# Query projections in the keys' form with evacuation by heads, and a reordered second row of the values, in a two-layer decoder trunk

## The chip, the cores and the metric

The kernel runs on one core of a Trainium2 chip. The metric is the device time of one execution in microseconds (us). Five engines work side by side, each through its own instructions in order: TensorE (PE, with its weight loads listed apart as PEld) for matrix products, ScalarE (ACT), VectorE (DVE), GpSimd (POOL) and SyncE (SP), which issues the loads. The trace gives the granted clock of TensorE as 0.998 of its full 2.4 GHz over the whole span.

## The reference, cut to what matters

Two pre-norm residual layers over 256 positions of width 1024: the first mixes tokens by attention with 8 heads of 128, the second by a causal pooling; each is followed by an MLP. With 256 positions there is one key block, so the attention is plain causal attention:

```
xn  = rms_norm(x, norm_mix[0])
q, k, v = split(xn @ w_qkv)          # 8 heads of 128 each
q, k = rotate the first 32 channels of each head by position (k likewise)
p   = softmax(mask(q @ k.T / sqrt(128)))
x   = x + (p @ v) @ w_o
x   = x + relu(rms_norm(x) @ w_up)**2 @ w_down
```

All inputs and outputs are float32.

## The kernel before

**Products in parts.** Each float32 matrix operand is split into a high part, rounded to the type that TensorE multiplies at full rate, and a low part, the rest. A product is three products: high by high, high by low, low by high. Weights come in slabs of 128x2048 (1 MB), each loaded by SyncE into one of three buffers `raw_*`, then split in pieces: ScalarE copies a piece (`wh_*`, line 177), VectorE subtracts (`wl_*`, line 181). `pump(n)` issues n such pieces, first the copy, then the subtraction; `pump_h` and `pump_l` issue the copies or the subtractions alone; `use(kind, j)` makes sure that a slab's pieces have been issued. After the last subtraction of a slab, the load of the slab three later is issued into the buffer that has come free. The slabs in order: four of the values, then for each of four pairs of heads keys and queries, then four of the output projection, then the MLP's.

**The order.** The order on each engine is written out by hand. What the program names first on an engine runs first there; between engines only data and buffers hold an instruction back.

**Values (lines 506 to 560).** Row k of eight: the tokens' channels k are transposed by TensorE (`transposes`), scaled into a high part by ScalarE and a low part by VectorE (lines 328, 333), and multiplied with row k of the value weights into four banks `dv`, 12 products of 512 columns. Within a row the steps run over (n, h): n is the kind of the three products, h the half of 512 columns. The dictionary `ahead` says at which row the transposes for later rows are issued.

**Attention (lines 588 to 756).** For each pair of heads j: the keys' products, their evacuation with the rotation, the scores of pair j - 1 (from the second pair on), then the queries' products, their evacuation, and the transposes of the probabilities of pair j - 1. The keys of pairs 1 to 3 are made by `wide_lo` and `wide_hi`: one head has a bank of its own, whose columns 0 to 255 take the products with the tokens' high part and 256 to 511 those with their low part, so that one product of 512 columns serves both; `key_evac` adds the halves. The queries, and the keys of pair 0, are made by `chan_block`: 24 products of 256 columns for each head, both heads in one bank; `qk_evac` shuffles the rotating channels into `sw` (line 598), multiplies the bank by the cosine table (599), `sw` by the sine table (601) and adds the two (602). Lines 601 and 602 run on VectorE for pair 0 and the queries of pair 1, on GpSimd otherwise.

**Scores and after.** `scores` (line 629) makes two score banks, adds the mask on VectorE (640), takes the exponentials on ScalarE (648), and scales the rows by the reciprocal sums: head 0 on ScalarE (656), head 1 on VectorE (659). `prob_t` transposes the probabilities on TensorE, `attend` multiplies them with the values; its result is split into `ah` (ScalarE, 709) and `al` (VectorE, 710). The score banks, the transposed probabilities and the results of `attend` take turns in two PSUM banks of tag "t": a bank is written again when its last reader is done. The queries' banks have the tag "u", also two.

Of the kernel before, what the change touches and what calls it, by code (L numbers as in the profile page):

```python
# [84 lines left out]
def tile_trunk(ctx: ExitStack, tc: tile.TileContext, x_in, positions, norm_mix, norm_mlp,  # L85
# [132 lines left out]
    def pump(n):  # L218
        for _ in range(n):
            hi_step()  # L220
            while lows:
                lo_step()
# [132 lines left out]
    def both(pair):  # L355
        pair[0]()
        pair[1]()
# [145 lines left out]
    nc.vector.tensor_scalar(xs[:, 0, 0:SEQ], t0[:, 0:SEQ], gcol[:, 0:1], None, op0=ALU.mult)  # L503
    lo()
    pump_h(1)
    ahead = {0: (1, 1), 1: (2, 2), 3: (4, 2)}
    for k in range(KT):
        wh, wl = use("v", k // 2, 99 if k % 2 else (2 if k < 4 else 1))
        ev = transposes(ahead[k][0], 0, "a", n=ahead[k][1]) if 0 < k and k in ahead else None
        steps = [(n, h) for n in range(3) for h in range(2)]  # L510
        if k == 0:
            steps.sort(key=lambda nh: nh[1])
        for n, h in steps:
            if k == 0 and (n, h) == (0, 1):
                both(transposes(1, 0, "a", n=1))
            hs = slice(h * HALF, (h + 1) * HALF)
            for s in range(NS):
                x0 = (SEQ if n == 1 else 0) + s * P
                w = wl if n == 2 else wh
                nc.tensor.matmul(dv[s, h], xs[:, k, x0:x0 + P], w[:, k % 2, hs],  # L520
                                 start=k == 0 and n == 0, stop=k == KT - 1 and n == 2)
# [1 line left out]
            block_split(6)  # L523
            block_split(7)
        if k < 7:
            pump(2 if k < 3 else 1)
        if k == 4:
            block_turn(6)
            block_turn(7)
# [63 lines left out]
    def qk_evac(nm, j, u):  # L593
        ct, st = tab[nm]
        t = work.tile([P, 2, SEQ], F32, tag="X", name="t_%s_%d" % (nm, j), bufs=4)
        sw = work.tile([ROT, 2, SEQ], F32, tag="sw", name="sw_%s_%d" % (nm, j), bufs=2)
        uv = u.rearrange("p (f t) -> p f t", f=2)
        nc.vector.stream_shuffle(sw.rearrange("p f t -> p (f t)"), u[0:ROT, :], swap)
        nc.vector.tensor_tensor(t, uv, ct.broadcast_to([P, 2, SEQ]), op=ALU.mult)
        e = nc.vector if j == 0 or (nm, j) == ("q", 1) else nc.gpsimd  # L600
        e.tensor_tensor(sw, sw, st.broadcast_to([ROT, 2, SEQ]), op=ALU.mult)
        e.tensor_tensor(t[0:ROT], t[0:ROT], sw, op=ALU.add)
        return t
# [5 lines left out]
    def key_evac(j, us):  # L609
# [10 lines left out]
        e.tensor_tensor(t, t, ct.broadcast_to([P, 2, SEQ]), op=ALU.mult)  # L620
        e.tensor_tensor(sw, sw, st.broadcast_to([ROT, 2, SEQ]), op=ALU.mult)
        e.tensor_tensor(t[0:ROT], t[0:ROT], sw, op=ALU.add)
        return t

    qk = {}
# [3 lines left out]
    def scores(j):  # L629
# [22 lines left out]
        for a in range(2):  # L652
            for b, (c0, c1) in enumerate(((0, P), (P, 3 * P))):
                i = 2 * a + b
                if a == 0:
                    nc.scalar.activation(pr[a][:, c0:c1], pr[a][:, c0:c1], AF.Copy,
                                         scale=sums[:, i:i + 1])
                else:
                    nc.vector.tensor_scalar(pr[a][:, c0:c1], pr[a][:, c0:c1],
                                            sums[:, i:i + 1], None, op0=ALU.mult)  # L660
        prob[j] = pr

    pts = {}
# [52 lines left out]
    for j in range(4):  # L716
# [24 lines left out]
            qk["k", j] = key_evac(j, us)  # L741
            scores(j - 1)
        w = use("q", j)
        u = qk_bank("q", j)
        chan_block(u, w, 0)
        pump(1 if j else 2)
        chan_block(u, w, 1)
        qk["q", j] = qk_evac("q", j, u)
        if j == 0:
            pump(1)  # L750
        if j == 3:
            nc.scalar.activation(vh, vsb[:, 0, HALF:D], AF.Copy)
            nc.vector.tensor_tensor(vl, vsb[:, 0, HALF:D], vh.bitcast(F32), op=ALU.subtract)
# [440 lines left out]
```

## Time and profile before

| | us |
|---|---|
| median of 3 runs | 484.26 |
| lowest, highest | 484.18, 484.8 |
| profiled execution | 484.62 |
| its span, first to last instruction | 482.5 |

The span is that of one execution in the hardware profiler. A page of the profile gives busy times of the engines, the span in slices, the chain of work that ended last, followed back from the last instruction, and groups of instructions by line. Beside the page the trace answers questions: timelines of an engine, tables of busy time by stretch, the chain in order of time, and waits. Matrix products are pipelined, and their ends are modelled: where products follow each other, the distance from start to start is what one costs. A name in a row is that of the program without its number, so `wl_k` stands for the keys' slabs of all pairs.

### The profile page before, as it was taken

How to read it: one execution, taken by the hardware profiler on the slowest of the kernel's cores; microseconds unless marked ns; L12 is line 12 of the kernel's file. 1: busy time of each engine (PE TensorE's matmuls, PEld its weight loads, DVE VectorE, ACT ScalarE, POOL GpSimd, SP SyncE). 2: the span in 40 equal slices, each digit the busy share in tenths (PEclk: the TensorE clock that was granted, in tenths of full speed). 3: DMA queues.
4: the chain of work that ended last, by engine and by line, in shares of the span. 5: the costliest groups of instructions: out<-in, count | busy, mean ns of one | idle time of the engine just before them, and what ended most of it. 6: DMA issues, size and time to landing. Idle time of an engine off the chain costs nothing.

```text
span 482.5 us, 6552 instructions
## 1 busy us (share of the span) xinstructions
PE 474.7 (98%) x2570; PEld 412.1 (85%) x2570; DVE 338.8 (70%) x498; ACT 255.1 (53%) x418; POOL 43.1 (9%) x41
## 2 busy tenths in 40 slices
PE   8999999999999999999999999999999999999994
PEld 7789999888888888888888889888888888888884
DVE  4789998955877484848566687778756557484745
ACT  4696665653686272635355554476535446272523
POOL 6910456300000000000000000000000000000000
PEclk9999999999999999999999999999999999999999
DMA  7986643480477758556573570078747472736202
GB/s 266 349 280 223 196 174 123 143 259 1 124 251 236 263 196 282 186 163 219 170 249 147 175 261 2 18 248 297 239 135 277 139 252 97 262 120 230 88 1 87
DMA packets 57342, 89.58 MB, mean 186 GB/s; under 512 B 2944, under 2 KB 46048, under 8 KB 57312
## 3 DMA queue, kind: packets, MB, share of 16 engines
q1 hardware_dynamic: 56896, 88.72, 55.1%
q8 instruction: 20, 0.33, 0.3%
q10 hardware_dynamic: 416, 0.45, 0.3%
q14 instruction: 10, 0.08, 0.0%
HBM read 88.11 MB, written 1.05 MB: 185 GB/s over the span
## 4 chain that ended last, share of the span: by engine, by line
PE 97%; DMA 1%; SPq 0%; ACT 0%; DVE 0%; issue 0%; ACTq 0%
PE u_m L432 24%; PE u_m L425 13%; PE d_m L401 12%; PE d_m L402 12%; PE d_m L403 12%; PE d_v L520 4%; PE k L432 2%; PE u_q L411 2%; PE u_q L410 2%; PE u_q L415 2%; PE d_o L401 2%; PE d_o L403 2%; PE d_o L402 2%; DMA xt<-in_x_dram 1%; PE k L425 1%; PE d_p L1066 1%
## 5 line engine op out<-in xcount | busy, mean ns | idle before, releaser
L432 PE MATMUL u_m<-xs,wh_u 128*128 128x512 f32 x512 | 122.1, 390 | 0.0
L432 PEld LDWEIGHTS u_m<-xs,wh_u 128*128 128x128 f32 x512 | 94.7, 188 | 18.8
L401 PE MATMUL d_m<-wh_d,hh 128*128 128x512 f32 x252 | 98.1, 389 | 0.0
L402 PE MATMUL d_m<-wl_d,hh 128*128 128x512 f32 x252 | 98.0, 389 | 0.0
L403 PE MATMUL d_m<-wh_d,hl 128*128 128x512 f32 x252 | 98.0, 389 | 0.0
L181 DVE TENSOR_TENSOR wl_d<-raw_d,wh_d 128x1024 fp32r<-128x1024 f32 x64 | 76.2, 1221 | 17.0 <-ACT wh_d L177 17.0
L181 DVE TENSOR_TENSOR wl_u<-raw_u,wh_u 128x1024 fp32r<-128x1024 f32 x64 | 75.8, 1222 | 12.2 <-ACT wh_u L177 12.2
L177 ACT ACTIVATE wh_d<-raw_d 128x1024 fp32r<-128x1024 f32 x64 | 64.7, 1046 | 21.7 <-DMA raw_d<-in_mlp_w_down_dram 21.7
L799 ACT ACTIVATE t<-u_m 128x256 f32<-128x256 f32 x64 | 24.0, 378 | 83.8 <-PE u_m L425 54.6
L177 ACT ACTIVATE wh_u<-raw_u 128x1024 fp32r<-128x1024 f32 x64 | 63.9, 1046 | 7.1 <-DMA raw_u<-in_mlp_w_up_dram 7.1
L425 PEld LDWEIGHTS u_m<-xs,wl_u 128*128 128x128 f32 x512 | 64.0, 191 | 1.4
L425 PE MATMUL u_m<-xs,wl_u 128*128 128x256 f32 x512 | 64.9, 283 | 0.0
L800 DVE TENSOR_TENSOR t<-u_m,t 128x256 f32<-128x256 f32 x64 | 26.5, 422 | 53.9 <-ACT t L799 53.2
L403 PEld LDWEIGHTS d_m<-wh_d,hl 128*128 128x128 f32 x252 | 47.3, 188 | 9.8
L401 PEld LDWEIGHTS d_m<-wh_d,hh 128*128 128x128 f32 x252 | 47.3, 188 | 9.8
L402 PEld LDWEIGHTS d_m<-wl_d,hh 128*128 128x128 f32 x252 | 47.3, 188 | 9.8
L810 ACT ACTIVATE hh<-hf 128x512 fp32r<-128x512 f32 x32 | 20.2, 633 | 45.0 <-DVE hf L809 45.0
L811 DVE TENSOR_TENSOR hl<-hf,hh 128x512 fp32r<-128x512 f32 x32 | 22.2, 692 | 22.5 <-ACT hh L810 22.5
L809 DVE SCALAR_TENSOR_TENSOR hf<-t 128x512 f32<-128x512 f32 x32 | 22.1, 692 | 1.1
L410 PE MATMUL u_q<-xs,wh_q 128*128 128x256 f32 x64 | 18.6, 291 | 0.0
L411 PE MATMUL u_q<-xs,wl_q 128*128 128x256 f32 x64 | 18.1, 283 | 0.0
L415 PE MATMUL u_q<-xs,wh_q 128*128 128x256 f32 x64 | 18.1, 283 | 0.0
(218 smaller groups left out, 554.8 us busy)
## 6 DMA issues: line engine op xcount, KB each, us to landing
raw_u<-in_mlp_w_up_dram SPq DMA_DIRECT2D x32, 1024.0 KB, 6.3
raw_d<-in_mlp_w_down_dram SPq DMA_DIRECT2D x32, 1024.0 KB, 4.8
raw_o<-in_attn_w_o_dram SPq DMA_DIRECT2D x4, 1024.0 KB, 4.8
raw_k<-in_attn_w_qkv_dram SPq DMA_DIRECT2D x4, 768.0 KB, 5.2
raw_q<-in_attn_w_qkv_dram SPq DMA_DIRECT2D x4, 768.0 KB, 4.8
raw_v<-in_attn_w_qkv_dram SPq DMA_DIRECT2D x2, 1024.0 KB, 9.0
raw_v<-in_attn_w_qkv_dram SPq DMA_DIRECT2D x3, 512.0 KB, 7.1
raw_k<-in_attn_w_qkv_dram SPq DMA_DIRECT2D x4, 256.0 KB, 5.4
```

The source lines that it names most:

```text
L177: nc.scalar.activation(wh[:, sl], src[:, sl], AF.Copy)
L181: nc.vector.tensor_tensor(wl[:, sl], src[:, sl], wh[:, sl].bitcast(F32), op=ALU.subtract)
L401: nc.tensor.matmul(acc, lh, wh, start=first, stop=False)
L402: nc.tensor.matmul(acc, lh, wl, start=False, stop=False)
L403: nc.tensor.matmul(acc, ll, wh, start=False, stop=last)
L410: nc.tensor.matmul(o, w[0][:, k, fs], hi, start=first, stop=False, skip_group_check=True)
L411: nc.tensor.matmul(o, w[1][:, k, fs], hi, start=False, stop=False, skip_group_check=True)
L415: nc.tensor.matmul(acc[:, f * SEQ:(f + 1) * SEQ], w[0][:, k, fs], xs[:, k, SEQ:2 * SEQ], start=False, stop=last, skip_group_check=True)
L425: nc.tensor.matmul(acc[:, 0:SEQ], w[1][:, k, f * P:(f + 1) * P], xs[:, k, 0:SEQ], start=first and k == 0, stop=not first and k == KT - 1, ...
L432: nc.tensor.matmul(acc, w[0][:, k, f * P:(f + 1) * P], xs[:, k, :], start=first and k == 0, stop=not first and k == KT - 1, skip_group_che ...
L799: nc.scalar.activation(t[:, ts], u[:, SEQ:2 * SEQ], AF.Copy)
L800: nc.vector.tensor_tensor(t[:, ts], u[:, 0:SEQ], t[:, ts], op=ALU.add)
```

## The change

It has five parts.

- Values: rows 0 and 1 both run their first half of columns (h = 0) before the second; the transposes for rows 2 and 3, issued ahead of row 1 before, are issued between row 1's halves, each into a bank of its own, with one weight piece (`pump(1)`) between their evacuations; one piece less is pumped after row 1.
- Keys of pair 0: the two operations of lines 601 and 602 go from VectorE to GpSimd. The queries of pair 0 keep theirs on VectorE.
- Queries of pairs 1 to 3: `wide_lo` and `wide_hi` into two banks of tag "u", instead of `chan_block`.
- Their evacuation, `query_evac`, works head by head: ScalarE copies the second half of the bank, VectorE adds the first, shuffles, and multiplies by the cosine table in SBUF; GpSimd does the sine product and the sum.
- The probabilities of head 1 are scaled by tensor_tensor with the reciprocal sum broadcast along the row, instead of tensor_scalar.

```diff
--- before.py
+++ after.py
@@ -503,16 +503,19 @@
     nc.vector.tensor_scalar(xs[:, 0, 0:SEQ], t0[:, 0:SEQ], gcol[:, 0:1], None, op0=ALU.mult)
     lo()
     pump_h(1)
-    ahead = {0: (1, 1), 1: (2, 2), 3: (4, 2)}
     for k in range(KT):
         wh, wl = use("v", k // 2, 99 if k % 2 else (2 if k < 4 else 1))
-        ev = transposes(ahead[k][0], 0, "a", n=ahead[k][1]) if 0 < k and k in ahead else None
+        ev = transposes(4, 0, "a") if k == 3 else None
         steps = [(n, h) for n in range(3) for h in range(2)]
-        if k == 0:
+        if k < 2:
             steps.sort(key=lambda nh: nh[1])
         for n, h in steps:
-            if k == 0 and (n, h) == (0, 1):
-                both(transposes(1, 0, "a", n=1))
+            if k < 2 and (n, h) == (0, 1):
+                pair = [transposes(a, 0, "a", n=1) for a in range(k + 1, 2 * k + 2)]
+                both(pair[0])
+                if k == 1:
+                    pump(1)
+                    both(pair[1])
             hs = slice(h * HALF, (h + 1) * HALF)
             for s in range(NS):
                 x0 = (SEQ if n == 1 else 0) + s * P
@@ -523,7 +526,7 @@
             block_split(6)
             block_split(7)
         if k < 7:
-            pump(2 if k < 3 else 1)
+            pump(2 if k in (0, 2) else 1)
         if k == 4:
             block_turn(6)
             block_turn(7)
@@ -597,7 +600,7 @@
         uv = u.rearrange("p (f t) -> p f t", f=2)
         nc.vector.stream_shuffle(sw.rearrange("p f t -> p (f t)"), u[0:ROT, :], swap)
         nc.vector.tensor_tensor(t, uv, ct.broadcast_to([P, 2, SEQ]), op=ALU.mult)
-        e = nc.vector if j == 0 or (nm, j) == ("q", 1) else nc.gpsimd
+        e = nc.vector if nm == "q" else nc.gpsimd
         e.tensor_tensor(sw, sw, st.broadcast_to([ROT, 2, SEQ]), op=ALU.mult)
         e.tensor_tensor(t[0:ROT], t[0:ROT], sw, op=ALU.add)
         return t
@@ -620,6 +623,20 @@
         e.tensor_tensor(t, t, ct.broadcast_to([P, 2, SEQ]), op=ALU.mult)
         e.tensor_tensor(sw, sw, st.broadcast_to([ROT, 2, SEQ]), op=ALU.mult)
         e.tensor_tensor(t[0:ROT], t[0:ROT], sw, op=ALU.add)
+        return t
+
+    def query_evac(j, us):
+
+        ct, st = tab["q"]
+        t = work.tile([P, 2, SEQ], F32, tag="X", name="t_q_%d" % j, bufs=4)
+        sw = work.tile([ROT, 2, SEQ], F32, tag="sw", name="sw_q_%d" % j, bufs=2)
+        for f in range(2):
+            nc.scalar.activation(t[:, f, :], us[f][:, SEQ:2 * SEQ], AF.Copy)
+            nc.vector.tensor_tensor(t[:, f, :], us[f][:, 0:SEQ], t[:, f, :], op=ALU.add)
+            nc.vector.stream_shuffle(sw[:, f, :], t[0:ROT, f, :], swap)
+            nc.vector.tensor_tensor(t[:, f, :], t[:, f, :], ct[:, 0, :], op=ALU.mult)
+            nc.gpsimd.tensor_tensor(sw[:, f, :], sw[:, f, :], st[:, 0, :], op=ALU.mult)
+            nc.gpsimd.tensor_tensor(t[0:ROT, f, :], t[0:ROT, f, :], sw[:, f, :], op=ALU.add)
         return t
 
     qk = {}
@@ -656,8 +673,9 @@
                     nc.scalar.activation(pr[a][:, c0:c1], pr[a][:, c0:c1], AF.Copy,
                                          scale=sums[:, i:i + 1])
                 else:
-                    nc.vector.tensor_scalar(pr[a][:, c0:c1], pr[a][:, c0:c1],
-                                            sums[:, i:i + 1], None, op0=ALU.mult)
+                    nc.vector.tensor_tensor(pr[a][:, c0:c1], pr[a][:, c0:c1],
+                                            sums[:, i:i + 1].broadcast_to([P, c1 - c0]),
+                                            op=ALU.mult)
         prob[j] = pr
 
     pts = {}
@@ -741,13 +759,23 @@
             qk["k", j] = key_evac(j, us)
             scores(j - 1)
         w = use("q", j)
-        u = qk_bank("q", j)
-        chan_block(u, w, 0)
-        pump(1 if j else 2)
-        chan_block(u, w, 1)
-        qk["q", j] = qk_evac("q", j, u)
         if j == 0:
+            u = qk_bank("q", j)
+            chan_block(u, w, 0)
+            pump(2)
+            chan_block(u, w, 1)
+            qk["q", j] = qk_evac("q", j, u)
             pump(1)
+        else:
+            us = [ps_u.tile([P, HALF], F32, tag="u", name="q_%d_%d" % (j, f)) for f in range(2)]
+            for f in range(2):
+                for k in range(KT):
+                    wide_lo(us[f], w, k, f)
+            pump(1)
+            for f in range(2):
+                for k in range(KT):
+                    wide_hi(us[f], w, k, f)
+            qk["q", j] = query_evac(j, us)
         if j == 3:
             nc.scalar.activation(vh, vsb[:, 0, HALF:D], AF.Copy)
             nc.vector.tensor_tensor(vl, vsb[:, 0, HALF:D], vh.bitcast(F32), op=ALU.subtract)
```

## Rows read from the trace of the kernel before

**Rows 1.** The page of the kernel before: one line of its first part (busy time, share of the span and instructions of each engine) and one of its fourth (the chain that ended last, by engine).
```profile
PE 474.7 (98%) x2570; PEld 412.1 (85%) x2570; DVE 338.8 (70%) x498; ACT 255.1 (53%) x418; POOL 43.1 (9%) x41
...
PE 97%; DMA 1%; SPq 0%; ACT 0%; DVE 0%; issue 0%; ACTq 0%
```

**Rows 2.** The table of stretches. Columns: the stretch, its length, busy time (and instructions) of PE, PEld, DVE, ACT and POOL, granted clock, DMA share, GB/s.
```profile
48.00:60.00 12.00, 12.00 (x91) 11.48 (x90) 11.48 (x25) 8.08 (x18) 4.93 (x3) 1.00 0.63 204
...
96.00:108.00 12.00, 12.00 (x63) 10.16 (x62) 6.77 (x8) 6.98 (x12) 0.00 (x0) 1.00 0.82 265
```

**Rows 3.** The timelines of TensorE, ScalarE, VectorE and TensorE's weight loads in the values' stage. Columns: start, length, engine, line, operation, what it writes from what, count, and in brackets the idle time before it and what ended it.
```profile
8.29 0.63 PE L520 MATMUL d_v<-wl_v,xs 128*128 128x512 f32 x2
9.46 0.63 PE L318 MATMUL tr_a<-ident,xt 128*128 128x128 f32 x4 [0.54 <-DMA xt<-in_x_dram]
...
8.14 1.15 ACT L177 ACTIVATE wh_v<-raw_v 128x512 fp32r<-128x512 f32 x2
...
16.90 1.06 ACT L177 ACTIVATE wh_v<-raw_v 128x1024 fp32r<-128x1024 f32 x1 [2.63 <-DMA raw_v<-in_attn_w_qkv_dram]
...
17.99 1.23 DVE L181 TENSOR_TENSOR wl_v<-raw_v,wh_v 128x1024 fp32r<-128x1024 f32 x1 [2.21 <-ACT wh_v L177]
19.13 0.87 DVE L333 SCALAR_TENSOR_TENSOR xs<-tr_a,gcol,xs 128x256 fp32r<-128x256 f32 x2
...
19.66 0.76 PEld L520 LDWEIGHTS d_v<-wh_v,xs 128*128 128x128 f32 x4 [0.16 <-DVE xs L333]
```

**Rows 4.** The chain that ended last, in order of time, from the second pair's keys to the third pair's. Columns: start, length, engine, what it writes, line, count.
```profile
42.27 1.92 PE k L425 x16
44.20 3.65 PE k L432 x16
...
48.73 0.43 PE s L637 x2
54.90 0.74 PE pt L670 x6
...
69.58 0.66 PE pt L670 x6
```

**Rows 5.** The timelines of VectorE and ScalarE around the first pair.
```profile
36.66 0.74 DVE L598 STREAM_SHUFFLE sw_k<-u_k 32x512 f32<-32x512 f32 x1
...
37.88 0.67 DVE L601 TENSOR_TENSOR sw_k<-sw_k,st_k 32x512 f32<-32x512 f32 x1
38.58 0.68 DVE L602 TENSOR_TENSOR t_k<-t_k,sw_k 32x512 f32<-32x512 f32 x1
39.19 2.34 DVE L181 TENSOR_TENSOR wl_k<-raw_k,wh_k 128x1024 fp32r<-128x1024 f32 x2
...
46.14 1.06 ACT L177 ACTIVATE wh_q<-raw_q 128x1024 fp32r<-128x1024 f32 x1 [4.20 <-DMA raw_q<-in_attn_w_qkv_dram]
```

**Rows 6.** The timelines of GpSimd and VectorE where both work (71 to 76 us, 87 to 91, 52 to 56), and VectorE with GpSimd idle (95.31).
```profile
71.29 1.28 POOL L601 TENSOR_TENSOR sw_q<-sw_q,st_q 32x512 f32<-32x512 f32 x1 [1.83 <-DVE sw_q L598]
72.65 2.15 POOL L602 TENSOR_TENSOR t_q<-t_q,sw_q 32x512 f32<-32x512 f32 x1
...
87.55 2.15 POOL L602 TENSOR_TENSOR t_q<-t_q,sw_q 32x512 f32<-32x512 f32 x1
...
71.80 4.09 DVE L181 TENSOR_TENSOR wl_o<-raw_o,wh_o 128x1024 fp32r<-128x1024 f32 x2
...
88.61 2.16 DVE L181 TENSOR_TENSOR wl_o<-raw_o,wh_o 128x1024 fp32r<-128x1024 f32 x1
...
52.52 2.27 POOL L621 TENSOR_TENSOR sw_k<-sw_k,st_k 32x512 f32<-32x512 f32 x1
...
53.77 1.38 DVE L659 TENSOR_SCALAR p<-p,sums 128x128 f32<-128x128 f32 x2
...
95.31 0.55 DVE L659 TENSOR_SCALAR p<-p,sums 128x128 f32<-128x128 f32 x2
```

**Rows 7.** GpSimd's timeline in the values' stage, one operation on 32x256.
```profile
16.57 0.72 POOL L481 TENSOR_TENSOR rot_a<-rot_a,rot_b 32x256 f32<-32x256 f32 x1
```

**Rows 8.** The timelines of VectorE, ScalarE and TensorE in the second pair.
```profile
49.68 0.74 DVE L616 TENSOR_TENSOR t_k<-k,t_k 128x256 f32<-128x256 f32 x2
...
57.29 0.72 DVE L598 STREAM_SHUFFLE sw_q<-u_q 32x512 f32<-32x512 f32 x1
...
59.82 1.21 DVE L181 TENSOR_TENSOR wl_k<-raw_k,wh_k 128x1024 fp32r<-128x1024 f32 x1
...
62.09 0.67 DVE L710 TENSOR_TENSOR al<-o,ah 128x512 fp32r<-128x512 f32 x1
...
55.42 0.84 ACT L681 ACTIVATE pts<-pt 128x384 f32<-128x384 f32 x2
...
63.02 0.39 PE L636 MATMUL s<-t_k,t_q 128*128 128x128 f32 x2
```

**Rows 9.** The timelines of VectorE and TensorE in the fourth pair and the first group of the output projection.
```profile
85.03 0.72 DVE L598 STREAM_SHUFFLE sw_q<-u_q 32x512 f32<-32x512 f32 x1
...
86.25 1.76 DVE L753 TENSOR_TENSOR v_parts<-vsb,v_parts 128x512 fp32r<-128x512 f32 x1
87.95 0.74 DVE L676 TENSOR_TENSOR ptp<-pt,ptp 128x256 fp32r<-128x256 f32 x2
...
88.80 0.60 PE L693 MATMUL o<-pts,vsb 128*128 128x128 f32 x4
```

## Prediction

> **What bounds the kernel now.** I read the page's busy shares and its chain of waits first: TensorE is busy for 98% of the span, and 97% of the chain that ended last is TensorE's own work [rows 1]. The reader should see that the change can gain only what TensorE no longer executes or no longer waits for, and that it loses whatever makes TensorE wait. Next the table of stretches: where queries, keys and scores are made VectorE is busy for 11.5 us of 12, against 6.8 us in the output projection that follows [rows 2]. So in exactly the stage that is changed a second engine has almost no idle time. Last I read the timelines of VectorE, GpSimd and TensorE there side by side, for what each handover between engines has to spare.
>
> **How the changed stage keeps time.** An operation of GpSimd and a VectorE operation with two SBUF inputs do not run together here. Two subtractions for `wl_o` take 4.09 us from 71.80 on, where GpSimd works, and two of the same size 2.34 us at 39.19, where it does not [rows 5, 6]. The times fit one behind the other: GpSimd's `sw_q` ends at 72.57, one subtraction (1.1) at 73.65, GpSimd's addition to `t_q`, in its queue since 72.65, at 74.80, and the second subtraction at 75.89. It repeats at 88.61: GpSimd ends at 89.70, the subtraction 1.07 later [rows 6]. So the engine that waits gets its turn after one instruction, and a GpSimd operation costs a VectorE that is never idle its whole length.
>
> By the Trainium skill ("SBUF — State Buffer", "Who interferes with whom") a VectorE instruction with two SBUF inputs and a GpSimd instruction that reads SBUF exclude each other for a whole instruction; the rows just named agree. That rule speaks against moving this work to GpSimd, as does the sum below, which is made from rows alone.
>
> **The change, part by part.**
>
> *Queries by 512-column products.* One pair takes 48 products of 256 columns now: from 49.16 (48.73 + 0.43) to 54.90, 5.74 us. The keys' form, which the queries take over, is 1.92 + 3.65 = 5.57 us [rows 4]. The columns stay the same, only issues fall away: 0.17 us per pair, three pairs, **-0.5 us**. This is on the path. Each pair now takes both banks of tag "u"; they last held the pair before, which is evacuated before its scores, so this costs nothing, and if it did it would show as a wait before the first product.
>
> *Values' second row by halves.* The path has a gap before 9.46: the last two products issue from 8.29 on at 0.23 us each (3.65 for 16), so TensorE could go on at about 8.75 and waits for x, 0.71 us [rows 3, 4]. The new order puts six products of row 1 there; their weight half is ready at about 8.7 (8.14, the first of two in 1.15). But 10 us later the path passes another point: `raw_v` of the third slab lands at 16.90; its copy, its subtraction (17.99, 1.23) and the low half of row 4 (19.13, the first of two, until 19.56) follow, and the weight load at 19.66 waits for just this [rows 3]. Nothing of that chain begins before the landing, so TensorE arrives earlier and waits longer. What survives is the spare there: 0 to 0.16 us; I take **0**. The moved transposes bring their ScalarE and VectorE operations and one weight piece with them, but no DMA: only a slab's last piece starts a load. They fall before 16.9, where both engines are idle for over 2 us [rows 3].
>
> *First keys' rotation to GpSimd.* VectorE loses 0.67 + 0.68 us (37.88, 38.58). GpSimd multiplies from about 37.5 (after the shuffle, 36.66 + 0.74) to 38.8, at 1.28 us; the first `wl_k` subtraction runs from 38.8 to 39.85; GpSimd's addition, waiting since 38.9, from 39.85 to 41.0; the second subtraction ends at 42.1 instead of 41.53 [rows 5, 6]. VectorE comes out 0.6 us later, not 1.3 earlier: **+0.6 us** off the path, into a queue without slack. The load that this subtraction releases (second queries, third pair) comes 0.6 us later too; ScalarE's copy waits for it until 46.14 and ends at 47.2, VectorE takes it up 1.2 us before its sum at 49.68, so 1.3 us cover it [rows 5, 8].
>
> *Probabilities by tensor_tensor.* The pair of tensor_scalar takes 1.38 us at 53.77, of which 1.02 is the wait for GpSimd's operation (52.52 + 2.27 = 54.79), and 0.55 us at 95.31 with GpSimd idle [rows 6]. Behind a wait 0.36 is left. No row shows a 128x128 tensor_tensor from SBUF; a sum of 128x256 takes 0.37 (49.68, two in 0.74) [rows 8], so the pair is 0.55 to 0.65, and the new second input lies in SBUF too. **+0.2 us** if it waits as now; bounds -0.7 (it doesn't wait for GpSimd at all) and +1.1 (GpSimd's next operation slips in between the two).
>
> *Evacuation by heads.* For the second pair VectorE now spends 57.29 to 59.82, 2.53 us. New: two sums of 0.37, two half shuffles of about 0.36 (half of 0.72), two products of about 0.38: 2.2 us [rows 8]. GpSimd gets four operations on 32x256. An undisturbed row of that size is 0.72 us, which is taken; the rows of 512 columns, 1.28, are the upper bound [rows 6, 7]. Of the four, two run beside VectorE's sums and shuffles, which read at most one SBUF input, and two hold up a product or a subtraction: 2 x 0.72 = 1.4 us. Together 3.65 against 2.53: **+1.1 us**. ScalarE gets two copies that wait for TensorE, each under the 0.42 us of a 384-column one; queued behind them are the transposed probabilities, which end at 56.26 now and are needed at 57.56 (54.90 + 0.74 + 1.92) [rows 4, 8]: 0.5 us stay to spare.
>
> **Where it reaches the path.** Behind the evacuation VectorE has two subtractions, `al` of the first pair and the keys' sums. `al` ends at 62.76 (62.09 + 0.67). It empties the bank that the second score product of the second pair writes, issued at 63.02 [rows 8]: 0.2 to 0.3 us to spare. VectorE's lateness there is 0.6 + 0.2 + 1.1 = 1.9 us, less 0.2: TensorE is about **+1.7 us** late. (Part of the same delay, not more of it, comes earlier, at the transposes at 54.90, which even now take 0.74 us against 0.66 later [rows 4].) From there VectorE is gated by TensorE, and the delay isn't paid twice. The two later pairs give back 2 x 0.17. In the fourth pair VectorE's `v_parts` and `ptp` (86.25, 87.95) close the bank that the products at 88.80 need, with 0.4 us to spare [rows 9]; the evacuation ahead of them (85.03 to 86.25) grows by 1.0 us and a wait of 0.7. VectorE waits for GpSimd there already (1.76 us for 512 columns), so I take a third of it, **+0.5 us** (0 to 1.2).
>
> Sum: +1.7 - 0.3 + 0.5 = **+1.9 us**. The profiled execution took 484.62 us with a span of 482.5, so 486.5 for its like; it lies 0.36 us above the median of the runs shown, 484.26, and I give the forecast for the median: **486.2 us**.
>
> **The rivals.** *Cover holds (same).* If GpSimd's half-size operations all run beside VectorE operations with one SBUF input, and the first keys' rotation costs nothing, TensorE keeps the -0.5 and the 0.08 at 54.90: 483.7. For it: the large subtractions split weights that are used only later, so some order of the two queues may hide all of it. Against it: 0.2 us of spare at 63.02. It decides at `al` of the first pair later by more than 0.2 us. *The gap at 9.46 is a real gain (faster).* If the third slab lands by 16.2 us rather than 16.90, the chain behind it ends 0.7 earlier and all 0.71 survives; with no new wait that is -0.71 - 0.5 - 0.08: 483.0. The loads ahead of it keep their order, so little speaks for it. *The broadcast doesn't wait for GpSimd.* Then the score chain gains 0.7 instead of losing 0.2, and the delay at 63.02 falls by 0.9: 485.3, at the border of no change and slower. Against it: every subtraction with two SBUF inputs waited [rows 6].
>
> **How the numbers follow.** A measurement of this kernel can tell about 0.2% (1.0 us) from no change. Chances: forecast 0.52 (+1.0 to +3.7, the upper end with nearer 1.2 us per GpSimd operation), cover holds 0.26, broadcast free 0.12 (half of it slower), gap gained 0.10. So slower 0.58, same 0.32, faster 0.10. The range runs from 483.4, just below "cover holds", to 488.2; it leaves out the faster case and the last tenth or so of mine.
>
> **What would show it.** Right: TensorE waiting for VectorE at the score products of the second pair, behind `al`; GpSimd busy some 6 us more; subtractions for `wl` in that stage longer than now; the weight load of row 4 still at 19.66; 5.57 us of TensorE per query pair. Wrong: that weight load 0.5 us earlier (the gap survives), probabilities' products of 0.3 us each while GpSimd works (no exclusion), or `al` of the first pair not later than 62.8 (cover holds).

## The result, and the profile after

| us | before | after |
|---|---|---|
| median, run side by side (6 runs each) | 484.5 | 487.59 |
| lowest, highest | 484.18, 484.97 | 487.0, 488.41 |
| profiled execution | 484.62 | 488.11 |
| its span | 482.5 | 486.3 |

The ratio is 1.0058, with a 95% interval from 1.0047 to 1.0068: 3.1 us slower, where the forecast was +1.9. The ratios in this document are not the quotients of the two medians beside them, and differ from those by up to 0.06%.

The first lines of the page and of its chain (the kernel after; engine, busy time, share, instructions; then the chain by engine):

```profile
PE 475.5 (98%) x2522; PEld 409.1 (84%) x2522; DVE 340.9 (70%) x509; ACT 256.9 (53%) x424; POOL 55.0 (11%) x51
...
PE 85%; DVE 8%; DMA 2%; ACT 1%; issue 1%; SPq 0%; DVEq 0%; ACTq 0%
```

TensorE has 48 instructions fewer than in [rows 1] and is busy no less. GpSimd is busy 11.9 us longer, twice the 6 us that were forecast; 6.18 us of its busy time are one operation on the first keys, which spends most of them waiting (`e3_keys0`, below). The chain that ended last is no longer TensorE's alone: 85% of it against 97%, and VectorE has 8%.

Where TensorE waits (the kernel after; line, what released it: total, times, longest, in us):

```profile
PE s L653 <- DVE al L728: 1.5, 2, 1.2
PE o L711 <- DVE ptp L694: 1.1, 1, 1.1
PE warm_up L298 <- DVE warm L237: 1.0, 1, 1.0
PE d_v L523 <- ACT wh_v L177: 0.8, 1, 0.8
```

The warm-up's wait stands in both kernels. New are the first two lines: score products of the second head wait for `al`, and the third `attend` waits for `ptp`. The wait for `x` after 8.29 [rows 3] has become one for the weights, `wh_v`, of 0.8 us: the six products moved there ran into the next late operand.

TensorE's timeline (the kernel after; start, length, and in brackets the idle time before it and what ended it):

```profile
49.63 2.25 PE L425 MATMUL q<-xs,wl_q 128*128 128x256 f32 x16
51.73 3.82 PE L432 MATMUL q<-xs,wh_q 128*128 128x512 f32 x16
55.39 1.01 PE L688 MATMUL pt<-ident,p 128*128 128x128 f32 x6
...
63.12 0.38 PE L653 MATMUL s<-t_k,t_q 128*128 128x128 f32 x2
...
65.17 0.46 PE L653 MATMUL s<-t_k,t_q 128*128 128x128 f32 x2 [1.24 <-DVE al L728]
...
80.09 0.46 PE L653 MATMUL s<-t_k,t_q 128*128 128x128 f32 x2 [0.26 <-DVE al L728]
...
92.44 0.71 PE L711 MATMUL o<-pts,vsb 128*128 128x128 f32 x4 [1.12 <-DVE ptp L694]
```

VectorE's timeline there (the kernel after), first the second pair, then the fourth:

```profile
58.05 0.41 DVE L635 TENSOR_TENSOR t_q<-q,t_q 128x256 f32<-128x256 f32 x1
...
58.51 0.43 DVE L636 STREAM_SHUFFLE sw_q<-t_q 32x256 f32<-32x256 f32 x1
58.97 0.43 DVE L637 TENSOR_TENSOR t_q<-t_q,ct_q 128x256 f32<-128x256 f32 x1
...
60.24 0.83 DVE L637 TENSOR_TENSOR t_q<-t_q,ct_q 128x256 f32<-128x256 f32 x1
61.00 1.75 DVE L181 TENSOR_TENSOR wl_k<-raw_k,wh_k 128x1024 fp32r<-128x1024 f32 x1
62.67 1.75 DVE L181 TENSOR_TENSOR wl_q<-raw_q,wh_q 128x1024 fp32r<-128x1024 f32 x1
64.35 0.68 DVE L728 TENSOR_TENSOR al<-o,ah 128x512 fp32r<-128x512 f32 x1
...
87.79 0.41 DVE L635 TENSOR_TENSOR t_q<-q,t_q 128x256 f32<-128x256 f32 x1
...
90.84 1.22 DVE L781 TENSOR_TENSOR v_parts<-vsb,v_parts 128x512 fp32r<-128x512 f32 x1
91.98 0.74 DVE L694 TENSOR_TENSOR ptp<-pt,ptp 128x256 fp32r<-128x256 f32 x2
```

GpSimd's (the kernel after), the four operations on the second pair's queries:

```profile
59.02 0.97 POOL L638 TENSOR_TENSOR sw_q<-sw_q,st_q 32x256 f32<-32x256 f32 x1 [1.97 <-DVE sw_q L636]
60.06 0.72 POOL L639 TENSOR_TENSOR t_q<-t_q,sw_q 32x256 f32<-32x256 f32 x1
60.76 0.91 POOL L638 TENSOR_TENSOR sw_q<-sw_q,st_q 32x256 f32<-32x256 f32 x1
61.74 1.59 POOL L639 TENSOR_TENSOR t_q<-t_q,sw_q 32x256 f32<-32x256 f32 x1
```

Read the last two together, second pair. The second cosine product starts at 60.24 and lasts 0.83 us, where the first lasts 0.43, and both subtractions last 1.75 instead of 1.21 [rows 8]: beside each of the three runs one GpSimd operation. The evacuation starts at 58.05 and `al` at 64.35, 6.30 us later; before, these were 57.29 and 62.09, 4.80 apart [rows 8]. TensorE would go on with the second score products at 63.8, 0.65 us behind the first as it did before, and goes on at 65.17.

The walk along TensorE shows where the time was lost. These are start times from the timelines of the two profiled executions:

| TensorE issues | before | after | after is later by |
|---|---|---|---|
| first product of the second pair's keys | 42.11 | 42.94 | 0.83 |
| first product of its queries | 48.81 | 49.63 | 0.82 |
| transposes behind them | 54.74 | 55.39 | 0.65 |
| second pair, scores of head 1 | 63.02 | 65.17 | 2.15 |
| transposes, next pair | 69.42 | 71.47 | 2.05 |
| third pair, scores of head 1 | 77.61 | 80.09 | 2.48 |
| transposes, next pair | 84.00 | 86.38 | 2.38 |
| third `attend` | 88.80 | 92.44 | 3.64 |
| fourth pair, scores | 91.33 | 95.08 | 3.75 |

From 42 us on that is 2.9 us, near the 3.1 of the medians. The 0.83 us ahead of it must not be counted, as the next lines show (the kernel after; ScalarE's copy of the third slab and TensorE's weight load of row 4):

```profile
17.67 1.06 ACT L177 ACTIVATE wh_v<-raw_v 128x1024 fp32r<-128x1024 f32 x1 [2.34 <-DMA raw_v<-in_attn_w_qkv_dram]
...
20.44 0.76 PEld L523 LDWEIGHTS d_v<-wh_v,xs 128*128 128x128 f32 x4 [0.44 <-DVE xs L333]
```

The slab landed 0.77 us later than in [rows 3], and all of values is late by that. It is nothing that the change did: in a kernel whose values are untouched (`e3_keys0`, below) the copy began at 17.63, and in the other runs at 15.72 to 17.78. One profiled execution is thus unsure by about a microsecond before the attention begins.

### The profile page after: what moved, and what is told of

Same layout as the page of the kernel before. It is cut to its first block, busy times and chain, and to the rows that moved or that the text cites. A ratio compares the mean times of both kernels' runs of the same rounds, so it can differ in the third digit from the quotient of the medians.

```text
span 486.3 us, 6494 instructions
## 1 busy us (share of the span) xinstructions
PE 475.5 (98%) x2522; PEld 409.1 (84%) x2522; DVE 340.9 (70%) x509; ACT 256.9 (53%) x424; POOL 55.0 (11%) x51
## 4 chain that ended last, share of the span: by engine, by line
PE 85%; DVE 8%; DMA 2%; ACT 1%; issue 1%; SPq 0%; DVEq 0%; ACTq 0%
PE u_m L432 24%; PE u_m L425 13%; PE d_m L402 12%; PE d_m L403 12%; PE d_m L401 12%; PE d_v L523 4%; DVE wl_o L181 2%; DVE wl_k L181 2%; DMA raw_v<-in_attn_w_qkv_dram 1%; PE d_o L401 1%; PE d_o L403 1%; PE d_o L402 1%; DVE wl_q L181 1%; DMA raw_q<-in_attn_w_qkv_dram 1%; PE d_p L1094 1%
## 5 line engine op out<-in xcount | busy, mean ns | idle before, releaser
L523 PE MATMUL d_v<-wh_v,xs 128*128 128x512 f32 x64 | 17.5, 406 | 0.8 <-ACT wh_v L177 0.8
L364 ACT ACTIVATE junk<-xt 128x512 f32<-128x512 f32 x15 | 9.5, 630 | 13.7 <-DVE xt L822 13.5
L523 PEld LDWEIGHTS d_v<-wh_v,xs 128*128 128x128 f32 x64 | 11.5, 189 | 4.3 <-ACT wh_v L177 1.8
```

## The experiments

**Theory.** Only the queries' evacuation costs time: it keeps VectorE longer, so `al` and `ptp` come late, and TensorE stands before the two banks of tag "t" that they must empty. **Rivals.** Other parts of the change have a share. Or it is the sharing of banks alone, so that with more banks the loss is gone. Or GpSimd's exclusion of VectorE is the price, so that without GpSimd there would be none. All medians stand beside runs of the kernel before on the same chip; "+" is slower.

**Each part alone** (before, with one part of the change). The values' order:

```diff
-        if k == 0:
+        if k < 2:
             steps.sort(key=lambda nh: nh[1])
...
-            pump(2 if k < 3 else 1)
+            pump(2 if k in (0, 2) else 1)
```

> Kernel before with the values' reordering alone. Theory A (the cost lies in the pairs 1 to 3, and the values' stage is paced by the landing of the third slab): no change, within 0.3 us of the kernel before, and the copy of the third slab begins at its landing in both. Rival (the new order itself makes the first loads or rows later, as the 0.78 us at the weight load of row 4 in the profile after suggest): about +0.8 us. Second rival (the gap at 9.46 is gained): -0.7 us.

485.07 against 484.97, ratio 1.0006 (0.9997 to 1.0014). Nothing, as forecast: the wait for `x` is gone, and one for the weights stands in its place. TensorE's timeline (this part alone):

```profile
9.38 1.20 PE L523 MATMUL d_v<-wh_v,xs 128*128 128x512 f32 x4 [0.53 <-ACT wh_v L177]
```

The queries' products and their evacuation, `chan_block` and `qk_evac` replaced for pairs 1 to 3:

```diff
+            us = [ps_u.tile([P, HALF], F32, tag="u", name="q_%d_%d" % (j, f)) for f in range(2)]
...
+            qk["q", j] = query_evac(j, us)
```

> Kernel before with the queries by 512-column products and the evacuation by heads alone. Theory A (VectorE and GpSimd take turns, al of the first pair and the bank of the third attend come late): -0.5 us of products, +1.2 at the second pair's scores, +0.3 at the third pair's, +1.0 at the third attend: about +2.0 us. Rival (it needs all three edits of the attention together to use up the spare): between -0.5 and +0.5 us.

488.04 against 484.97, ratio 1.0069 (1.0055 to 1.0082), +3.1: the whole loss of the change, and more than the +2.0 expected of this part. TensorE's timeline (this part alone; the two waits):

```profile
64.18 0.46 PE L650 MATMUL s<-t_k,t_q 128*128 128x128 f32 x2 [1.24 <-DVE al L724]
...
91.19 0.71 PE L707 MATMUL o<-pts,vsb 128*128 128x128 f32 x4 [0.98 <-DVE ptp L690]
```

The two large waits of the whole change are here again, 1.24 and 0.98 us against 1.24 and 1.12; only its small third one, 0.26 at 80.09, is not. With the other parts at nothing, above and in the next two runs, that settles the first rival.

The first keys' rotation on GpSimd:

```diff
-        e = nc.vector if j == 0 or (nm, j) == ("q", 1) else nc.gpsimd
+        e = nc.vector if nm == "q" else nc.gpsimd
```

> Kernel before with the first keys' rotation on GpSimd alone. The prediction's term: VectorE 0.6 us later, +0.3 to +0.4 us at the second pair's scores. Theory A as the profile after has it (GpSimd waits behind four subtractions, VectorE comes out about 0.3 us earlier): 0, within 0.2 us.

484.69 against 484.97, ratio 0.9997 (0.9988 to 1.0006): nothing. The edit does more than its name says: in the kernel before, the queries of the third and fourth pairs pass this line too, so their sine product and sum go from GpSimd back to VectorE. Until 71 us, though, the trace has the first keys' part alone, and it costs nothing there either: from the second pair's first key product (42.90) to the third pair's queries (64.18) TensorE takes 21.28 us, before 21.38. But that is not by the mechanism of the prediction. The timelines of ScalarE, GpSimd and VectorE (this run):

```profile
17.63 1.06 ACT L177 ACTIVATE wh_v<-raw_v 128x1024 fp32r<-128x1024 f32 x1 [2.89 <-DMA raw_v<-in_attn_w_qkv_dram]
...
38.27 6.18 POOL L601 TENSOR_TENSOR sw_k<-sw_k,st_k 32x512 f32<-32x512 f32 x1 [2.66 <-DVE sw_k L598]
...
38.69 2.34 DVE L181 TENSOR_TENSOR wl_k<-raw_k,wh_k 128x1024 fp32r<-128x1024 f32 x2
40.95 2.34 DVE L181 TENSOR_TENSOR wl_q<-raw_q,wh_q 128x1024 fp32r<-128x1024 f32 x2
...
45.16 1.67 DVE L602 TENSOR_TENSOR t_q<-t_q,sw_q 32x512 f32<-32x512 f32 x1
```

GpSimd's sine product begins 0.42 us before VectorE's first subtraction and yet lasts 6.18 us. The four subtractions are as long as undisturbed ones, 2.34 for two, and end at 43.29; the sine product ends 1.16 us behind them, at 44.45, about its own length. VectorE is not held up here at all; it pays later, in line 602 at 45.16, which lasts 1.67 instead of 0.68, since it comes beside GpSimd's addition. The two nearly cancel: VectorE's subtractions behind it start at 46.76, 9.31 us after the shuffle at 37.45; before, they were 9.61 apart. The later queries say the same from the other side: in the third pair VectorE takes 4.82 us from the shuffle (71.16) to `al` (75.98) with their rotation on itself, and took 5.33 (70.48, 75.81) with it on GpSimd.

The probabilities by tensor_tensor:

```diff
-                    nc.vector.tensor_scalar(pr[a][:, c0:c1], pr[a][:, c0:c1],
-                                            sums[:, i:i + 1], None, op0=ALU.mult)
+                    nc.vector.tensor_tensor(pr[a][:, c0:c1], pr[a][:, c0:c1],
+                                            sums[:, i:i + 1].broadcast_to([P, c1 - c0]), op=ALU.mult)
```

> Kernel before with the probabilities of head 1 scaled by tensor_tensor alone. Theory A (the operation with a broadcast second input waits for GpSimd as the old one did and takes 0.15 us more): 0 to +0.3 us, the pair at about 1.5 us. Rival (the broadcast does not contend): pair at 0.6 us, -0.1 us in all.

485.14 against 484.97, ratio 0.9999 (0.9991 to 1.0008): nothing. VectorE's and GpSimd's timelines (this part alone; the pair, and GpSimd's operation beside it):

```profile
53.41 1.51 DVE L659 TENSOR_TENSOR p<-p,sums 128x128 f32<-128x128 f32 x2
...
52.15 2.28 POOL L621 TENSOR_TENSOR sw_k<-sw_k,st_k 32x512 f32<-32x512 f32 x1
```

The pair takes 1.51 us against 1.38 [rows 6] and ends when it may: GpSimd's operation, which began at 52.15, ends at 54.43, and the pair at 54.92, half a microsecond behind it. So the broadcast operand doesn't free it of GpSimd; the third case of the prediction falls.

**The rotation left out** (the kernel after, with shuffles, sine products and sums of the queries of pairs 1 to 3 left out):

```diff
-            nc.vector.stream_shuffle(sw[:, f, :], t[0:ROT, f, :], swap)
...
-            nc.gpsimd.tensor_tensor(sw[:, f, :], sw[:, f, :], st[:, 0, :], op=ALU.mult)
-            nc.gpsimd.tensor_tensor(t[0:ROT, f, :], t[0:ROT, f, :], sw[:, f, :], op=ALU.add)
```

> The changed kernel without the rotation of the queries of pairs 1 to 3: their shuffle, sine product and sum are left out, so that GpSimd has nothing to do for them and VectorE two operations less per pair. Theory A (all of the loss is in what the evacuation puts on VectorE and in its waits for GpSimd): VectorE gets back 0.9 + 1.6 us a pair, TensorE no longer waits, and the 0.5 us of the shorter products show: 484.0 to 484.6 us. Rival (the wide products or the use of both banks cost by themselves): 486 us or more.

483.89 against 484.41, ratio 0.9990 (0.9981 to 0.9998): 0.5 us faster than before, and TensorE's products have no wait in the whole stage. VectorE's timeline (without the rotation; start of the evacuation, and `al`):

```profile
56.93 0.41 DVE L634 TENSOR_TENSOR t_q<-q,t_q 128x256 f32<-128x256 f32 x1
...
60.78 0.69 DVE L724 TENSOR_TENSOR al<-o,ah 128x512 fp32r<-128x512 f32 x1
```

3.85 us from one to the other, where the whole evacuation has 6.30. So the shorter products are worth their 0.5 us, as soon as VectorE is not late, and neither they nor the two banks cost anything by themselves. It is not shown by this that the rotation is what the change added: the kernel before has one too and takes 4.80 us, so VectorE has less to do here than it had then. The next run tells more.

**The rotation on VectorE alone** (the kernel after, without GpSimd in the queries of pairs 1 to 3):

```diff
-            nc.gpsimd.tensor_tensor(sw[:, f, :], sw[:, f, :], st[:, 0, :], op=ALU.mult)
-            nc.gpsimd.tensor_tensor(t[0:ROT, f, :], t[0:ROT, f, :], sw[:, f, :], op=ALU.add)
+            nc.vector.tensor_tensor(sw[:, f, :], sw[:, f, :], st[:, 0, :], op=ALU.mult)
+            nc.vector.tensor_tensor(t[0:ROT, f, :], t[0:ROT, f, :], sw[:, f, :], op=ALU.add)
```

> The changed kernel with the sine product and the sum of the queries' evacuation on VectorE, so that GpSimd does nothing for these queries. Theory A (each GpSimd operation holds VectorE up for about its own length, 1.6 us a pair, and four operations of about 0.4 us on VectorE cost the same): within 0.7 us of the changed kernel. Rival one (the waits for GpSimd are the cost, the added operations are small): 1 to 2 us faster. Rival two (VectorE's own operations are the cost, the waits lie beside others): 1.5 to 3 us slower.

487.88 against 484.41, ratio 1.0075 (1.0062 to 1.0088), +3.5; the whole change had +3.1, and the two intervals overlap. VectorE's timeline (rotation on VectorE; the two sums with the shuffles behind them, first subtraction, `al`):

```profile
57.41 0.41 DVE L635 TENSOR_TENSOR t_q<-q,t_q 128x256 f32<-128x256 f32 x1
57.87 0.42 DVE L636 STREAM_SHUFFLE sw_q<-t_q 32x256 f32<-32x256 f32 x1
...
59.45 0.41 DVE L635 TENSOR_TENSOR t_q<-q,t_q 128x256 f32<-128x256 f32 x1
...
59.90 0.43 DVE L636 STREAM_SHUFFLE sw_q<-t_q 32x256 f32<-32x256 f32 x1
...
61.48 1.20 DVE L181 TENSOR_TENSOR wl_k<-raw_k,wh_k 128x1024 fp32r<-128x1024 f32 x1
...
63.75 0.67 DVE L728 TENSOR_TENSOR al<-o,ah 128x512 fp32r<-128x512 f32 x1
```

The evacuation lasts 4.07 us instead of 2.95, and the two subtractions take 1.20 again instead of 1.75; from start to `al` it is 6.34 us, against 6.30. So GpSimd relieves VectorE of nothing here: its four operations take 1.5 us from VectorE (0.40 in the second cosine product, 0.54 in each subtraction), and would cost 1.5 there (4.07 less 2.55). The third rival falls in its strict form: without GpSimd the loss is the same. And since the second pair's rotation was on VectorE before too, this run shows what the change adds: 4.07 us against 2.53 [rows 8], of which the two sums, from their starts to those of the shuffles, are 0.9; the other four operations, done in halves, take the remaining 3.2 where they took 2.53 whole.

**The attend results in banks of their own** (the kernel after; the first two in banks of the values, the third in one of tag "u"):

```diff
-        o = ps_t.tile([P, HALF], F32, tag="t", name="o_%d" % j)
+        if j < 2:
+            o = ps_d.tile([P, HALF], F32, tag="d0%d" % j, name="o_%d" % j)
+        elif j == 2:
+            o = ps_u.tile([P, HALF], F32, tag="u", name="o_%d" % j)
```

> The changed kernel with attend's results of the first three pairs in banks of their own (the free key banks for pairs 0 and 1, a queries' bank for pair 2), so that neither a score product nor the third attend waits for al or for ptp through a bank. Theory A (VectorE is saturated from 49 to 92 us; the bank is only where its lateness shows): 0.3 to 0.8 us faster than the changed kernel, about 487 us, and TensorE waits for VectorE elsewhere (probabilities' transposes, v_parts). Rival (the bank's order alone is the cost, VectorE could be late without harm): 2.7 us faster, 485 us or less.

486.52 against 484.41, ratio 1.0039 (1.0024 to 1.0053), +2.1: by the medians about 1.0 us of the 3.1 is gone, by the traces of the two kernels 0.8, where 0.3 to 0.8 was expected. The waits for `al` and for `ptp` before the third `attend` are gone too, but two of the 3.1 us stay. TensorE's timeline (own banks; the third transposes and the products behind `v_parts`):

```profile
83.89 1.31 PE L688 MATMUL pt<-ident,p 128*128 128x128 f32 x6
...
91.16 1.07 PE L723 MATMUL o<-ptp,v_parts 128*128 128x256 f32 x5 [1.26 <-DVE v_parts L786]
```

The delay comes up at the next places where TensorE meets VectorE: the transposes last 1.31 us instead of 0.82, and the values' low products wait 1.26 for `v_parts`. So the banks are where the lateness is paid first, not what makes it; the second rival falls.

**Lighter, in the old order** (before, with the queries' part, the banks of the run above, and both heads' scaling on ScalarE):

```diff
-                if a == 0:
+                if a < 2:
                     nc.scalar.activation(pr[a][:, c0:c1], pr[a][:, c0:c1], AF.Copy,
```

> Kernel before with the queries' part of the change, attend's results in banks of their own, and the probabilities of both heads scaled on ScalarE, which takes the pair of 1.4 us (with its wait) from VectorE. Theory A: VectorE gets back about what the evacuation by heads takes from it, and TensorE keeps most of the shorter products: 0.5 us faster to 0.7 us slower than the kernel before. Rival (a late VectorE isn't what costs): 3 us slower like the queries' part alone.

487.20 against 484.41, ratio 1.0062 (1.0049 to 1.0076), +2.8. The expectation missed by 2 us or more, and the time is the one that its rival named; what the trace shows is still a late VectorE, and a late ScalarE with it. VectorE's and TensorE's timelines, and one wait of TensorE's weight loads from 40 to 100 us (this kernel; in the last line the total, times and longest):

```profile
57.71 1.23 DVE L181 TENSOR_TENSOR wl_k<-raw_k,wh_k 128x1024 fp32r<-128x1024 f32 x1 [2.51 <-ACT wh_k L177]
...
92.81 1.07 PE L719 MATMUL o<-ptp,v_parts 128*128 128x256 f32 x5 [1.24 <-DVE v_parts L782]
...
PEld pt L684 <- ACT p L670: 1.2, 5, 0.3
```

VectorE lost the pair of 1.4 us [rows 6], but the time did not come free for it: the next subtraction needs ScalarE's copy of the same piece, and this copy now stands behind four scalings instead of two. VectorE sat idle for 2.51 us in each pair, and TensorE waits 1.24 us for `v_parts`, as with the pair on VectorE (1.26, the run above). ScalarE's two added scalings cost too: the transposes of the probabilities wait for it 1.2 us in all. Work taken from an engine helps only if what stands behind it in its queue could begin earlier.

**The same, with another order** (the kernel above; the copy of a second piece ahead of the exponentials, its subtraction thus free of ScalarE, `v_parts` made with the third pair's scores, and the first keys' rotation on GpSimd):

```diff
-        pump_h(1)
+        if j == 2:
+            nc.scalar.activation(vh, vsb[:, 0, HALF:D], AF.Copy)
+        pump_h(2 if j < 3 else 1)
...
         nc.vector.reciprocal(sums, sums)
+        if j == 2:
+            nc.vector.tensor_tensor(vl, vsb[:, 0, HALF:D], vh.bitcast(F32), op=ALU.subtract)
...
-            pump(1)
+            pump_l(1)
```

> The run with its own banks and scaling on ScalarE, with three more edits: the second weight piece of a queries' stage is copied ahead of the exponentials and subtracted right after the reciprocal (where VectorE sat idle for 2.5 us a pair, waiting for that copy behind the scaling), v_parts is made in the same gap of pair 2's scores, and the first keys' rotation is on GpSimd. Theory A: VectorE's lateness at al and at v_parts is gone, TensorE keeps the shorter products but for some 0.3 us at the first probabilities: 0 to 0.5 us faster than the kernel before. Rival (the shorter products can't be had, something else in the evacuation paces TensorE): 1 us or more slower than the kernel before.

484.23 against 485.06, ratio 0.9984 (0.9975 to 0.9993): 0.8 us faster than before, more than the 0.5 expected at most, and so faster than both kernels. By the traces 0.45 us of it lies in this stage: from the second pair's first key product to the fourth pair's scores it is 48.77 us (41.57 to 90.34), before 49.22. TensorE's products have no wait in the stage, its weight loads one of 0.4 us, for `ptp`, and one of 0.2, for the probabilities. VectorE's timeline (this kernel; second pair, and `v_parts`):

```profile
54.82 0.42 DVE L632 TENSOR_TENSOR t_q<-q,t_q 128x256 f32<-128x256 f32 x1 [1.82 <-ACT t_q L631]
...
57.78 3.42 DVE L181 TENSOR_TENSOR wl_k<-raw_k,wh_k 128x1024 fp32r<-128x1024 f32 x2
61.12 0.68 DVE L733 TENSOR_TENSOR al<-o,ah 128x512 fp32r<-128x512 f32 x1
...
81.02 1.25 DVE L669 TENSOR_TENSOR v_parts<-vsb,v_parts 128x512 fp32r<-128x512 f32 x1
```

Here VectorE is ready ahead of TensorE: it waits 1.82 us for ScalarE's copy from the queries' bank until 54.82, `al` starts at 61.12, and `v_parts` is made at 81.02, 3.4 us ahead of the fourth pair's evacuation (84.41). One subtraction of the stage has slid behind it (the twentieth from the first pair's on starts at 96.80, before at 93.97), into the output projection, where VectorE has 5 of 12 us to spare [rows 2]. Four edits were made at once, so that it works is shown, and not which of them carries how much.

**A head start for GpSimd** (before, with the edit of `e3_keys0`, that on the later queries included, and one extra copy of 512 columns out of PSUM on VectorE between shuffle and cosine product):

```diff
+        if (nm, j) == ("k", 0):
+            spare = work.tile([P, HALF], F32, tag="junk", name="spare", bufs=1)
+            nc.vector.tensor_copy(spare, u)
         nc.vector.tensor_tensor(t, uv, ct.broadcast_to([P, 2, SEQ]), op=ALU.mult)
```

> Kernel before with the first keys' rotation on GpSimd, and one more copy of 128x512 from PSUM on VectorE ahead of its cosine product, whose result nobody reads; it gives GpSimd's first operation a start of about 1.0 us instead of 0.42 us ahead of VectorE's subtractions. Theory A (the engine that starts first holds the pair, the prediction's term): GpSimd's sine product takes about 1.3 us, the first subtraction waits for it, and its addition gets in behind one subtraction. Rival (subtractions that follow each other without a gap always keep GpSimd out): GpSimd's sine product takes over 5 us again. Time in both cases within 0.5 us of the kernel before.

485.33 against 485.06, ratio 1.0010 (1.0000 to 1.0019): within what can be told from no change. GpSimd's and VectorE's timelines (with the extra copy):

```profile
37.23 1.29 POOL L604 TENSOR_TENSOR sw_k<-sw_k,st_k 32x512 f32<-32x512 f32 x1 [2.78 <-DVE sw_k L598]
38.60 2.16 POOL L605 TENSOR_TENSOR t_k<-t_k,sw_k 32x512 f32<-32x512 f32 x1
...
38.24 3.61 DVE L181 TENSOR_TENSOR wl_k<-raw_k,wh_k 128x1024 fp32r<-128x1024 f32 x2
```

Now that the sine product begins 1.0 us ahead of the subtractions, it takes 1.29 us, and GpSimd's addition goes between the two subtractions, which take 3.61 instead of 2.34. This is the course that the prediction had drawn for the change itself, on the same two operations.

## Why the prediction was right, and where it was off

The direction, the stage, the engine and the place were right: TensorE waits at the second pair's scores behind `al`, VectorE's subtractions there are longer, nothing came of the gap in the values. The size was 1.9 against 3.1 us. By its terms:

- **Queries' products, -0.5.** Right. From the queries' first product to the transposes is 5.76 us against 5.93, 0.17 less in each pair, and the run without the rotation is 0.5 us faster.
- **Values by halves, 0.** Right, by the part alone; the reason given, that TensorE arrives earlier at row 4 and waits longer there, shows in one trace of the new order, that with the rotation on VectorE: the third slab's copy starts at 16.96, and the weight load of row 4 waits 0.59 us, until 19.79. In the changed kernel and in the part alone the gap was lost at once, to the wait for `wh_v` of 0.82 and 0.53 us, and the part alone has no wait at row 4 at all. The late weight load of the changed kernel is that of one execution.
- **First keys on GpSimd, +0.6 off the path.** Wrong in the mechanism. It was reasoned that the engine that waits gets its turn after one instruction; here GpSimd waited for four. VectorE came out some 0.3 us earlier. As no time hung on it alone, the sum did not suffer much: 0.6 us of the 1.9 of lateness at `al` did not exist.
- **Probabilities by tensor_tensor, +0.2.** Right: +0.13, and it does wait for GpSimd.
- **Evacuation by heads, +1.1.** Too small: 6.30 against 4.80 us from its start to `al`, +1.5. GpSimd's part was right: 1.5 us in sum, 1.4 was forecast. The six operations themselves take 2.55 us (2.95 less 0.40), not 2.2: half an operation costs more than half, 0.43 for a half shuffle against 0.72 for a whole one.
- **At `al`, +1.7.** Measured 1.40 (2.15 less 0.75 from the scores' first product, 63.12 against 62.37). Two errors of opposite sign, the 0.6 that wasn't and the 0.4 that was missing; that the term came so near is partly luck.
- **"The delay isn't paid twice."** Wrong in the third pair: there TensorE loses another 0.4 us at the same point, 80.09, with `al` late again.
- **The fourth pair, +0.5.** This is the step that failed, with most of the missing time: 1.26 measured (3.64 less 2.38 in the table), above its bound of 1.2. The evacuation ahead of `v_parts` takes 3.05 us (87.79 to 90.84) where it took 1.22 [rows 9]. That is +1.83, and 1.0 with a wait of 0.7 had been written; 0.42 of it is that wait, in the second cosine product, and 1.41 are operations. So the sum of the two was near, less the 0.4 of spare 1.3. What failed is that only a third was taken, because VectorE waits for GpSimd there already: of that old wait no more than 0.54 us came back, `v_parts` going from 1.76 to 1.22, and the evacuation starts 0.38 late besides. 1.83 - 0.54 + 0.38 less the 0.4 of spare is the measured delay, to 0.01 us.

Of the cases that were set beside the forecast, "cover holds" fell with the spare at 63.02, as its own condition said; "gap gained" with the values' part alone; and "the broadcast doesn't wait" with the pair at 53.41.

## What to carry over

When two engines exclude each other, count a move between them as no relief: here a rotation on GpSimd or on VectorE kept VectorE for 6.30 or 6.34 us. On an engine without slack, count a stage's operations pair by pair, since the same edit can replace four operations in one pair and two in the next: the evacuation itself grew by 0.4 us in the second pair, where it replaced four, and by 1.8 in the fourth, where it replaced two. And before taking work from a busy engine, look at what its next instruction waits for: the scaling moved away left 2.51 us of idle time per pair, until the copy in front of it was moved too.

## What the hardware showed beside this

How GpSimd and VectorE take turns is less even than one row suggests. With VectorE's subtractions following each other without a gap, GpSimd's operation got in between two of them where it had been queued while the first waited for GpSimd itself: its addition at 61.74 lasts 1.59 us and fits between 61.00's and 62.67's subtraction, and with the extra copy the addition at 38.60 (2.16 us) fits behind a subtraction that took 1.37 us instead of 1.20. It was shut out for four of them, 6.18 us in all, where it began 0.42 us ahead and the first subtraction didn't wait; six kernels that had the edit without the extra copy show it, with 6.17 or 6.18 us. The head start doesn't decide it by its length alone: in the kernel before, the sine product of the fourth pair's queries also began 0.42 us ahead, of `v_parts` (85.83 against 86.25 [rows 9]), and there VectorE waited, with 1.76 us for `v_parts` instead of the 0.67 that it takes in `e3_keys0` with GpSimd idle. Which condition decides was not settled, and a start in the timeline need not be the moment at which an engine first reads.

By the Trainium skill ("SBUF — State Buffer", "Who interferes with whom") the engine that issues first holds the shared pair of ports for the whole instruction, and the other is fully blocked. The runs agree on whole instructions, with 1.75 us for a subtraction that takes 1.20 without GpSimd; the operation that began first and lasted 6.18 us does not agree with it, by the start times that the trace gives.
